# Hard-max attention on one core: the order of the first loads and the way the first transposes leave PSUM

## Chip, cores and metric

One of the eight cores of a Trainium2 chip runs the kernel. The metric is the device time of one execution in microseconds. A ratio is the mean time of one kernel's fast runs over the mean of the other's of the same rounds, so it is not quite the ratio of the medians that are quoted beside it; the bracket behind a ratio is its 95% interval.

The engines are called by their short names: PE multiplies matrices into the memory PSUM, ACT, DVE and POOL work on tiles, ACT and DVE copy results out of PSUM here, and POOL also issues the loads. The head is the time up to the first fold (explained below), the ramp the few tiles after it, the body the long stretch in which DVE is nearly always busy, the tail what follows the last fold. A landing is the moment at which a load has arrived.

## The reference, cut to what matters

```python
B, Sq, Sk, D = 4, 4096, 4096, 128            # all float32
def reference(q, k, v):
    logits = np.matmul(q, k.transpose(0, 2, 1))
    best = np.argmax(logits, axis=-1)         # one key per query
    return v[b_idx, best, :]
```

For each of 16,384 queries the kernel finds the key with the largest dot product and returns that key's row of v.

## The kernel before

The 16,384 queries are 128 tiles of 128. For each tile PE multiplies the transposed queries (`qT`) with the transposed keys (`kT`), in fp16. The keys stand in groups of four, and `kT` holds sums and differences of neighbours: `u` = 0 and 2 are sums, 1 and 3 differences. So |difference| + sum gives the larger of a pair (doubled), and 4096 keys shrink to 1024 group bounds. Per tile ACT takes two absolute values out of PSUM (`A`) and one scaled ReLU (`E`). DVE folds the last part with `E` into `W` (the fold) and then takes the eight largest. Later stages gather the three differences of the best group, decide between its four keys, and gather v.

q and k are loaded with a cast from fp32 to fp16, transposed by PE against an identity and copied out of PSUM. The identity is made on POOL, its fp16 forms `identh` and `identn` (its negative) on DVE. Before that PE runs warm-up matmuls on zeros, while the first loads are under way.

```python
pp = tc.tile_pool(name="ps", bufs=4, space=PSUM)      # four buffers of 1024 fp32 columns, for everything
# ... (cut)
for h in range(2):
    load_k(0, h, 0, 16)          # 2048 keys each, 512 KB written
load_q(0, 0, 8)                  # 8 query tiles
load_q(0, 8, NQT)                # the other 24
# ... 16 warm-up matmuls, make_identity, identh, identn (cut)
for h in range(2):
    put_k(0, h)                  # DVE: differences to the first key of each group; store of 384 KB as k16
# ... constants: three long iotas on POOL, iota_r, then on DVE:
nc.vector.tensor_copy(out=iota_h, in_=iota_r)

def trn_half(b, u, h):           # 8 matmuls of 128 columns
    # ... ps = tk_t[u], one 1024-column tile for both halves; o = ps[:, h * 512 + m * P: ...]
    if h == 1:
        nc.scalar.activation(out=kT[b % 2][:, u * 1024:(u + 1) * 1024], in_=ps, func=AF.Copy)

for u in (1, 3, 0, 2):
    trn_half(0, u, 0)            # fills all four PSUM buffers
trn_half(0, 1, 1)
trn_q(0, 0)                      # eight transposes and one 1024-column copy on ACT
trn_half(0, 3, 1)
trn_half(0, 0, 1)
dpart(0, 0)                      # pd = qT * kT[1]; ACT: A = |pd|
trn_half(0, 2, 1)
dpart(0, 1)
```

Each engine has its own instructions in this program order, and in the timelines below it works through them in that order.

Of the kernel before, what the change touches and what calls it, by code (L numbers as in the profile page):

```python
# [7 lines left out]
FP32 = mybir.dt.float32  # L8
# [8 lines left out]
AF = mybir.ActivationFunctionType  # L17
# [10 lines left out]
def kernel(ctx, tc, q, k, v, out):  # L28
    nc = tc.nc
    B, Sq, D = q.shape  # L30
    Sk = k.shape[1]
    P = 128
    NQT = Sq // P
# [10 lines left out]
    pp = ctx.enter_context(tc.tile_pool(name="ps", bufs=4, space=bass.MemoryType.PSUM))  # L44
# [10 lines left out]
    kT = [bp.tile([P, Sk], FP16, name=f"kT{i}", tag=f"kT{i}") for i in range(2)]  # L55
    qT = [bp.tile([P, Sq], FP16, name=f"qT{i}", tag=f"qT{i}") for i in range(2)]
    natk = [bp.tile([P, 2, 16, P], FP16, name=f"natk{i}", tag=f"natk{i}") for i in range(2)]
    kd = bp.tile([P, 2, 4, 3, P], FP16, name="kd", tag="kd")
    natq = [bp.tile([P, NQT, P], FP16, name=f"natq{i}", tag=f"natq{i}") for i in range(2)]

    def load_k(b, h, x, y):
        kb = k[b].rearrange("(h p n) d -> p h n d", p=P, n=16)
        nc.gpsimd.dma_start(out=natk[b % 2][:, h, x:y], in_=kb[:, h, x:y])  # L63

    def load_q(b, x, y):
        nc.gpsimd.dma_start(out=natq[b % 2][:, x:y], in_=q[b].rearrange("(p t) d -> p t d", p=P)[:, x:y])  # L66

    def put_k(b, h):
        if b >= B:
            return  # L70
        src = natk[b % 2][:, h].rearrange("p (g f) d -> p g f d", f=4)
        nc.vector.tensor_tensor(out=kd[:, h], in0=src[:, :, 1:4, :], in1=src[:, :, 0:1, :].to_broadcast([P, 4, 3, P]),
                                op=OP.subtract)
        kb16 = k16[b].rearrange("(h p n) d -> p h (n d)", p=P, n=4)
        nc.sync.dma_start(out=kb16[:, h], in_=kd[:, h].rearrange("p g f d -> p (g f d)"))

    def load_part(b, i):
        if b >= B:
            return
        if i < 8:  # L80
            load_k(b, i // 4, i % 4 * 4, i % 4 * 4 + 4)
        else:
            load_q(b, (i - 8) * NQT // 8, (i - 7) * NQT // 8)

    for h in range(2):
        load_k(0, h, 0, 16)
    load_q(0, 0, 8)
    load_q(0, 8, NQT)

    wz = cp.tile([P, 512], FP16, tag="wz")  # L90
    nc.vector.memset(wz, 0.0)
    for i in range(2):
        ps = pp.tile([P, 1024], FP32, tag="u", name=f"warm_{i}")
        for j in range(8):
            nc.tensor.matmul(out=ps[:, (j % 2) * 512:(j % 2 + 1) * 512], lhsT=wz[:, 0:P], rhs=wz, start=True, stop=True)

    ident = cp.tile([P, P], FP32, tag="ident")
    masks.make_identity(nc, ident)
    identh = cp.tile([P, P], FP16, tag="identh")
    nc.vector.tensor_copy(out=identh, in_=ident)  # L100
    identn = cp.tile([P, P], FP16, tag="identn")
    nc.vector.tensor_scalar(out=identn, in0=ident, scalar1=-1.0, scalar2=None, op0=OP.mult)
    for h in range(2):
        put_k(0, h)
    D_t = [cp.tile([P, 8, 4], FP32, name=f"D{i}", tag=f"D{i}") for i in range(3)]
    for D in D_t:
        nc.vector.memset(D, 0.0)
# [33 lines left out]

    tk_t = {}

    def trn_half(b, u, h):
        x = 2 * (u // 2)
        if h == 0:
            tk_t[u] = pp.tile([P, 1024], FP32, tag="u", name=f"tk_{b}_{u}")
        ps = tk_t[u]
        for m in range(4):
            o = ps[:, h * 512 + m * P:h * 512 + (m + 1) * P]  # L150
            nc.tensor.matmul(out=o, lhsT=natk[b % 2][:, h, 4 * m + x, :], rhs=identh, start=True, stop=False)
            nc.tensor.matmul(out=o, lhsT=natk[b % 2][:, h, 4 * m + x + 1, :],
                             rhs=identn if u % 2 else identh, start=False, stop=True)
        if h == 1:
            nc.scalar.activation(out=kT[b % 2][:, u * 1024:(u + 1) * 1024], in_=ps, func=AF.Copy)

    def unit_k(b, i):
        h, u, y = i // 8, i // 2 % 4, i % 2
# [10 lines left out]
    def turn_q(b, x, y):  # L169
        nc.sync.dma_start_transpose(out=qT[b % 2][:, x * P:y * P].rearrange("p (t r) -> p t r", r=P),  # L170
                                    in_=natq[b % 2][:, x:y, :].rearrange("p t d -> p (t d)"))

    def trn_q(b, g):
        if b >= B:
            return
        ps = pp.tile([P, 1024], FP32, tag="u", name=f"tq_{b}_{g}")
        for i in range(8):
            nc.tensor.matmul(out=ps[:, i * P:(i + 1) * P], lhsT=natq[b % 2][:, g * 8 + i, :], rhs=identh,
                             start=True, stop=True)
        nc.scalar.activation(out=qT[b % 2][:, g * 1024:(g + 1) * 1024], in_=ps, func=AF.Copy)  # L180

    E_t = {}
    A_t = {}
# [8 lines left out]
    def dpart(t, x):  # L192
        if t >= T:
            return
        ps = pp.tile([P, 1024], FP32, tag="u", name=f"pd_{t}_{x}")
        mm(ps, t, 1 + 2 * x, True)
        A = ep.tile([P, 1024], FP16, tag=f"A{x}", name=f"A_{t}_{x}")
        nc.scalar.activation(out=A, in_=ps, func=AF.Abs)  # L198
        A_t[t, x] = A
# [16 lines left out]
    def screen(t):  # L216
        dpart(t, 0)
        spart(t - 1, 0)
        dpart(t, 1)
        spart(t - 1, 1)  # L220

    def fold(t):
        E, ps = E_t.pop(t)
        nc.vector.scalar_tensor_tensor(out=W_t[t % NW].bitcast(I16)[:, 1::2], in0=ps, scalar=QSCALE, in1=E,  # L224
                                       op0=OP.mult, op1=OP.max)

    def top(t):
        nc.vector.max(out=TOP[:, t, :], in_=W_t[t % NW].bitcast(FP32))  # L228
# [338 lines left out]
    def all_rows():  # L567
# [4 lines left out]
        with tc.If(left > 0):  # L572
            for b in range(B):
                with tc.For_i(0, NQT, 1) as t:
# [13 lines left out]
                    nc.gpsimd.indirect_dma_start(out=vv, out_offset=None, in_=v_flat, in_offset=IOA(ap=win, axis=0))  # L588
                    nc.sync.dma_start(out=out[b].rearrange("(p t) d -> p t d", p=P)[:, bass.ds(t, 1), :].rearrange("p o d -> p (o d)"), in_=vv)

    for u in (1, 3, 0, 2):
        trn_half(0, u, 0)
    trn_half(0, 1, 1)
    trn_q(0, 0)
    trn_half(0, 3, 1)
    trn_half(0, 0, 1)
    dpart(0, 0)
    trn_half(0, 2, 1)
    dpart(0, 1)
    cuts = list(range(0, T - 16 + 1, 8)) + [T - x for x in (12, 8, 4, 0)]  # L600
    chunks = list(zip(cuts[:-1], cuts[1:]))
# [28 lines left out]
    def step(it):  # L630
        waiting = [s for s in live if s["kind"] == "dots" and ready(s, it)]
        quota = 2 if len(waiting) > 1 else 1
        for s in list(live):
            if s["kind"] == "dots":
                if quota and advance(s, it, False):
                    quota -= 1
            else:
                advance(s, it, False)
# [11 lines left out]
    def issue(it):  # L650
        n = 0
        while near_q and (n < 1 or near_q[0] in marks):
            g = near_q.pop(0)
            n += g not in marks
            g()
        if fast and it >= rest[0]:
            fast.pop(0)()
            rest[0] = it + 3
        take_late(2 if n == 0 and len(late_q) > 4 or it >= T - 8 and it % 2 else 1)

    def gathers(t):
        for c, (t0, t1) in enumerate(chunks):
            if t0 <= t < t1 and ((t - t0) % 2 or t == t1 - 1):
                x = t0 + (t - t0) // 2 * 2
                gather(c, x, t - x + 1)
            if t == t0:
                start(pick(c, t0, t1), "pick", c)
        if t % 8 == 7:
            put_rec(t - 7, t + 1)
        if t == SEGS[1] - 1:  # L670
            last = [c for c, x in enumerate(chunks) if x[1] == t + 1][0]
            start(flag_segment(0, t + 1, lambda: ("cnt", last) in done, lambda: ("out", last) in done), "flags")

    units = []
    for b in range(1, B):
        x = b * NQT
        units += [(x - 1, x - NQT + 8 + 3 * i // 2, unit_k, b, i) for i in range(16)]
    for it in range(T):
        b, qt = it // NQT, it % NQT
        if 2 <= qt < 10:  # L680
            load_part(b + 1, qt - 2)
        elif 10 <= qt < 18:
            load_part(b + 1, qt - 2)
        open_units = [u for u in units if u[1] <= it]
        if open_units:
            u = min(open_units)
            units.remove(u)
            assert it <= u[0]
            u[2](*u[3:])
        if it in (1, 2, 3):  # L690
            turn_q(0, it * 8, it * 8 + 8)
        elif qt >= 16 and qt % 2 == 0 and b + 1 < B:
            turn_q(b + 1, (qt - 16) * 2, (qt - 14) * 2)
        if it > 0:
            screen(it)
        if it >= 1:
            fold(it - 1)
        if it % NQT in (9, 13):
            put_k(it // NQT + 1, it % NQT // 13)
        step(it)  # L700
        if it >= 2:
            top(it - 2)
        if it >= 3:
            gathers(it - 3)
        step(it)
        issue(it)
# [72 lines left out]
```

## Time and profile before

| | before |
|---|---|
| median of 4 runs | 474.54 us (474.13 to 474.59) |
| span of the profiled run | 472.4 us |
| first `A` on ACT, first `E` on ACT, first fold on DVE | 14.79, 18.40, 19.53 us |
| last (128th) fold | 419.06 us |

First, the table of engines by stretch of the kernel before. After the stretch and its length come busy microseconds and instruction counts (x) of PE, PEld, DVE, ACT and POOL, then the granted clock, the DMA share and GB/s.

```profile
12.00:24.00 12.00, 10.48 (x63) 4.89 (x61) 3.02 (x3) 11.94 (x14) 0.95 (x2) 1.00 1.02 204
...
36.00:100.00 64.00, 61.46 (x310) 28.03 (x310) 63.03 (x107) 63.49 (x80) 34.47 (x40) 1.00 0.45 89
100.00:200.00 100.00, 91.48 (x444) 40.66 (x442) 98.31 (x175) 93.24 (x110) 72.75 (x81) 1.00 0.54 115
200.00:300.00 100.00, 89.65 (x443) 40.09 (x442) 98.17 (x193) 90.95 (x109) 71.27 (x79) 1.00 0.53 113
300.00:400.00 100.00, 90.61 (x394) 37.62 (x393) 100.00 (x208) 91.80 (x99) 69.53 (x70) 1.00 0.30 86
```

The second stretch belongs to the head: ACT is busy 11.94 of 12 us and DVE 3.02. From 36 to 100 us ACT and DVE are both nearly full, and from 100 us on DVE is busy 98 to 100%. So the head is paced by ACT and what feeds it, and the body by DVE.

Now the head by time. The timeline of ACT in the kernel before gives start and duration in us, line, operation and shapes; in brackets stand the idle time before it and what ended it.

```profile
9.87 1.02 ACT L155 ACTIVATE kT<-tk 128x1024 f16<-128x1024 f32 x1 [7.85 <-PE tk L152]
12.06 1.02 ACT L180 ACTIVATE qT<-tq 128x1024 f16<-128x1024 f32 x1 [1.17 <-PE tq L178]
12.98 1.94 ACT L155 ACTIVATE kT<-tk 128x1024 f16<-128x1024 f32 x2
14.79 1.04 ACT L198 ACTIVATE A<-pd 128x1024 f16<-128x1024 f32 x1
15.69 1.06 ACT L155 ACTIVATE kT<-tk 128x1024 f16<-128x1024 f32 x1
...
18.40 1.10 ACT L211 ACTIVATE E<-psn 128x1024 int16<-128x1024 f32 x1
```

And from the timelines of PE and of DVE in the same run:

```profile
11.40 0.62 PE L178 MATMUL tq<-identh,natq 128*128 128x128 f16 x8 [1.57 <-DMA natq<-in_q_dram]
```
```profile
6.60 0.96 DVE L72 TENSOR_TENSOR kd<-natk 128x1536 f16<-128x1536 f16 x1 [1.01 <-DMA natk<-in_k_dram]
9.01 1.05 DVE L72 TENSOR_TENSOR kd<-natk 128x1536 f16<-128x1536 f16 x1 [1.45 <-DMA natk<-in_k_dram]
...
10.10 1.29 DVE L126 CAST iota_h<-iota_r 128x128 f16<-128x128 f32 x1
19.53 1.31 DVE L224 SCALAR_TENSOR_TENSOR W<-psn,E 128x1024 int16<-128x1024 f32 x1 [8.14 <-ACT E L211]
```

k half 1 is there at 9.01 (the second DVE line waited for its landing). PE then waits for q until 11.40. From 12.06 ACT never rests: qT, three copies of 1024 columns, and the first `A` before the last of them. Five copies of about 1 us each pass through ACT, four of them after q's landing. DVE does nothing for 8.14 us before its first fold.

### The profile page before, as it was taken

How to read it: one execution, taken by the hardware profiler on the slowest of the kernel's cores; microseconds unless marked ns; L12 is line 12 of the kernel's file. 1: busy time of each engine (PE TensorE's matmuls, PEld its weight loads, DVE VectorE, ACT ScalarE, POOL GpSimd, SP SyncE). 2: the span in 40 equal slices, each digit the busy share in tenths (PEclk: the TensorE clock that was granted, in tenths of full speed). 3: DMA queues.
4: the chain of work that ended last, by engine and by line, in shares of the span. 5: the costliest groups of instructions: out<-in, count | busy, mean ns of one | idle time of the engine just before them, and what ended most of it. 6: DMA issues, size and time to landing. Idle time of an engine off the chain costs nothing. (4 is left out here: it accounts for less than half of the span.)

```text
span 472.4 us, 6274 instructions
## 1 busy us (share of the span) xinstructions
PE 381.7 (81%) x1840; PEld 168.9 (36%) x1840; DVE 417.8 (88%) x845; ACT 380.7 (81%) x438; POOL 305.6 (65%) x345
## 2 busy tenths in 40 slices
PE   7899999999898889999888979999999889920000
PEld 4444444443343334443333434443333333300000
DVE  4288999999999999999999999999999999998400
ACT  1999999999998899999998889999999888920000
POOL 9025544666787876666878765667777567777740
PEclk9999999999999999999999999999999999975555
DMA  7914564143455946242666736142333132324320
GB/s 134 211 32 87 108 115 93 56 119 63 119 94 125 193 87 147 57 124 65 134 133 156 113 108 97 55 114 65 118 89 109 52 94 58 110 73 121 98 82 5
DMA packets 40777, 47.43 MB, mean 100 GB/s; under 512 B 24200, under 2 KB 32395, under 8 KB 40736
## 3 DMA queue, kind: packets, MB, share of 16 engines
q0 software_dynamic: 18464, 30.97, 31.1%
q1 hardware_dynamic: 22272, 16.00, 12.8%
q8 instruction: 15, 0.25, 0.2%
q14 instruction: 26, 0.21, 0.2%
HBM read 39.59 MB, written 12.19 MB: 110 GB/s over the span
## 5 line engine op out<-in xcount | busy, mean ns | idle before, releaser
L198 ACT ACTIVATE A<-pd 128x1024 f16<-128x1024 f32 x256 | 259.1, 1046 | 18.3 <-PE pd L189 17.8
L245 POOL DMA_INDIRECT kg<-k,cand x128 | 127.2, 994 | 103.9 <-DVE p L264 25.0
L224 DVE SCALAR_TENSOR_TENSOR W<-psn,E 128x1024 int16<-128x1024 f32 x128 | 166.4, 1300 | 15.1 <-ACT E L211 12.1
L189 PE MATMUL pd<-kT,qT 128*128 128x512 f16 x512 | 152.1, 378 | 17.4 <-ACT A L198 15.5
L189 PE MATMUL psn<-kT,qT 128*128 128x512 f16 x512 | 151.8, 377 | 15.4 <-ACT A L198 10.8
L189 PEld LDWEIGHTS <-qT 128*128 128x128 f16 x1024 | 98.4, 97 | 166.1 <-issue 77.9
L228 DVE MAX8 TOP<-W 128x8 f32<-128x1024 f32 x128 | 156.2, 1220 | 0.0
L208 PE MATMUL psn<-A,identh 128*128 128x512 f16 x512 | 152.0, 378 | 0.0
L302 POOL DMA_INDIRECT vr<-in_v_dram,win x128 | 125.5, 980 | 39.0 <-issue 35.0
L211 ACT ACTIVATE E<-psn 128x1024 int16<-128x1024 f32 x128 | 132.8, 1038 | 6.7 <-PE psn L208 5.9
L208 PEld LDWEIGHTS <-identh 128*128 128x128 f16 x512 | 49.5, 97 | 60.8
L260 DVE TENSOR_TENSOR prod<-kg,natq 128x768 f16<-128x768 f16 x64 | 35.0, 549 | 1.5 <-DMA kg<-k,cand 1.5
L264 DVE TENSOR_TENSOR p<-prod 128x384 f16<-128x384 f16 x64 | 22.3, 350 | 0.0
L269 DVE TENSOR_REDUCE D<-p 128x6 f32<-128x192 f16 x64 | 21.4, 338 | 0.0
L167 ACT ACTIVATE kT<-uk 128x256 f16<-128x256 f32 x48 | 20.0, 416 | 0.9 <-PE uk L164 0.9
L163 PE MATMUL uk<-identh,natk 128*128 128x128 f16 x96 | 15.8, 218 | 0.6 <-ACT A L198 0.6
L63 POOL DMA_DIRECT2D natk<-in_k_dram x26 | 15.7, 604 | 0.9 <-POOLq L763 0.8
L267 DVE TENSOR_TENSOR p<-p 128x192 f16<-128x192 f16 x64 | 15.7, 247 | 0.0
L66 POOL DMA_DIRECT2D natq<-in_q_dram x26 | 15.4, 594 | 0.1
L460 PE MATMUL fp_e<-n_e,tri 128*128 128x1 f32 x2 | 0.6, 362 | 16.4 <-DVE n_e L458 16.4
L164 PEld LDWEIGHTS <-natk 128*128 128x128 f16 x96 | 9.3, 97 | 7.7 <-issue 5.5
L163 PEld LDWEIGHTS <-natk 128*128 128x128 f16 x96 | 9.3, 97 | 5.6
(148 smaller groups left out, 142.4 us busy)
## 6 DMA issues: line engine op xcount, KB each, us to landing
out_dram<-vr SPq DMA_DIRECT2D x14, 512.0 KB, 3.2
k<-kd SPq DMA_DIRECT2D x8, 384.0 KB, 4.5
natk<-in_k_dram POOLq DMA_DIRECT2D x24, 128.0 KB, 3.8
natq<-in_q_dram POOLq DMA_DIRECT2D x24, 128.0 KB, 3.3
kg<-k,cand POOLq DMA_INDIRECT x128, 2.7
vr<-in_v_dram,win POOLq DMA_INDIRECT x128, 2.5
natk<-in_k_dram POOLq DMA_DIRECT2D x2, 512.0 KB, 7.0
out_dram<-vr SPq DMA_DIRECT2D x4, 256.0 KB, 2.3
```

The costliest lines, as they stand in the source:

```text
L163: nc.tensor.matmul(out=o, lhsT=natk[b % 2][:, h, 4 * m + x, :], rhs=identh, start=True, stop=False)
L189: nc.tensor.matmul(out=ps[:, n * 512:(n + 1) * 512], lhsT=qT[b % 2][:, qt * P:(qt + 1) * P], rhs=kT[b % 2][:, u * 1024 + n * 512:u * 1024 ...
L198: nc.scalar.activation(out=A, in_=ps, func=AF.Abs)
L208: nc.tensor.matmul(out=ps[:, n * 512:(n + 1) * 512], lhsT=identh, rhs=A[:, n * 512:(n + 1) * 512], start=False, stop=True)
L211: nc.scalar.activation(out=E, in_=ps, func=AF.Relu, scale=QSCALE)
L224: nc.vector.scalar_tensor_tensor(out=W_t[t % NW].bitcast(I16)[:, 1::2], in0=ps, scalar=QSCALE, in1=E, op0=OP.mult, op1=OP.max)
L228: nc.vector.max(out=TOP[:, t, :], in_=W_t[t % NW].bitcast(FP32))
L245: near_q.append(lambda j=j: nc.gpsimd.indirect_dma_start(out=kg[:, j].rearrange("p f d -> p (f d)"), out_offset=None, in_=k16[t0 // NQT], ...
L260: nc.vector.tensor_tensor(out=prod, in0=kg, in1=natq[b % 2][:, x - b * NQT:x - b * NQT + m, :].unsqueeze(2).to_broadcast([P, m, 3, P]), op ...
L264: nc.vector.tensor_tensor(out=p1, in0=prod[:, :, :, 0:64], in1=prod[:, :, :, 64:128], op=OP.add)
L269: nc.vector.tensor_reduce(out=d[:, x - c0:x - c0 + m, 1:4], in_=p2, axis=AX_X, op=OP.add)
L302: late_q.append(lambda j=j: nc.gpsimd.indirect_dma_start(out=vr[:, j, :], out_offset=None, in_=v_flat, in_offset=IOA(ap=win[:, j:j + 1], a ...
```

## The change

Its intent: let the first tile's scores start earlier. Only four query tiles stay in the first q load, and it comes between the two halves of k. Each half of a key column block leaves PSUM by itself, as 512 columns, on ACT or on DVE. The second store of key differences moves behind the first fold, and two warm-up matmuls go.

```diff
-    for h in range(2):
-        load_k(0, h, 0, 16)
-    load_q(0, 0, 8)
-    load_q(0, 8, NQT)
+    load_k(0, 0, 0, 16)
+    load_q(0, 0, 4)
...
-        for j in range(8):            # per warm-up tile, two tiles
+        for j in range(7):
...
     masks.make_identity(nc, ident)
+    load_k(0, 1, 0, 8)
+    load_k(0, 1, 8, 16)
+    load_q(0, 4, 8)
+    load_q(0, 8, NQT)
...
-    for h in range(2):
-        put_k(0, h)
...
-    for u in (1, 3, 0, 2):
-        trn_half(0, u, 0)
-    trn_half(0, 1, 1)
-    trn_q(0, 0)
-    trn_half(0, 3, 1)
-    trn_half(0, 0, 1)
-    dpart(0, 0)
-    trn_half(0, 2, 1)
-    dpart(0, 1)
+    trn_half(1, 0, ALL, by_act)       # each: 512 columns, copied out at once
+    trn_half(3, 0, ALL, by_dve)
+    trn_half(0, 0, ALL, by_act)
+    trn_q(0, 4, by_dve)
+    trn_half(2, 0, ALL, by_act)
+    put_k(0, 0)
+    for u in (1, 3, 0, 2):
+        trn_half(u, 1, (0, 1))        # first part of k half 1
+    trn_half(1, 1, (2, 3), by_act)
+    trn_half(3, 1, (2, 3), by_dve)
+    dpart(0, 0)
+    trn_half(0, 1, (2, 3), by_dve)
+    trn_half(2, 1, (2, 3), by_dve)
+    dpart(0, 1)
...                                    # in the loop over tiles, at tile 1:
+            turn_q(0, 4, 8)            # the q tiles 4 to 7, by a DMA transpose
+            put_k(0, 1)                # behind the first fold
```

More of the change, by code (lines that the diff above doesn't have):

```diff
@@ L142, with trn_half, by_act, by_dve @@
     tk_t = {}
-    def trn_half(b, u, h):
+    def trn_half(u, h, ms, put=None):
         x = 2 * (u // 2)
-        if h == 0:
-            tk_t[u] = pp.tile([P, 1024], FP32, tag="u", name=f"tk_{b}_{u}")
+        if ms[0] == 0:
+            tk_t[u] = pp.tile([P, 512], FP32, tag="u", name=f"tk_{u}_{h}")
         ps = tk_t[u]
-        for m in range(4):
-            o = ps[:, h * 512 + m * P:h * 512 + (m + 1) * P]
-            nc.tensor.matmul(out=o, lhsT=natk[b % 2][:, h, 4 * m + x, :], rhs=identh, start=True, stop=False)
-            nc.tensor.matmul(out=o, lhsT=natk[b % 2][:, h, 4 * m + x + 1, :],
+        for m in ms:
+            o = ps[:, m * P:(m + 1) * P]
+            nc.tensor.matmul(out=o, lhsT=natk[0][:, h, 4 * m + x, :], rhs=identh, start=True, stop=False)
+            nc.tensor.matmul(out=o, lhsT=natk[0][:, h, 4 * m + x + 1, :],
                              rhs=identn if u % 2 else identh, start=False, stop=True)
-        if h == 1:
-            nc.scalar.activation(out=kT[b % 2][:, u * 1024:(u + 1) * 1024], in_=ps, func=AF.Copy)
+        if put is not None:
+            put(kT[0][:, u * 1024 + h * 512:u * 1024 + h * 512 + 512], ps)
+    def by_act(dst, src):
+        nc.scalar.activation(out=dst, in_=src, func=AF.Copy)
+    def by_dve(dst, src):
+        nc.vector.tensor_copy(out=dst, in_=src)
     def unit_k(b, i):
@@ L171, in turn_q, with trn_q @@
                                     in_=natq[b % 2][:, x:y, :].rearrange("p t d -> p (t d)"))
-    def trn_q(b, g):
-        if b >= B:
-            return
-        ps = pp.tile([P, 1024], FP32, tag="u", name=f"tq_{b}_{g}")
-        for i in range(8):
-            nc.tensor.matmul(out=ps[:, i * P:(i + 1) * P], lhsT=natq[b % 2][:, g * 8 + i, :], rhs=identh,
+    def trn_q(x, y, put):
+        ps = pp.tile([P, 512], FP32, tag="u", name=f"tq_{x}")
+        for i in range(x, y):
+            nc.tensor.matmul(out=ps[:, (i - x) * P:(i - x + 1) * P], lhsT=natq[0][:, i, :], rhs=identh,
                              start=True, stop=True)
-        nc.scalar.activation(out=qT[b % 2][:, g * 1024:(g + 1) * 1024], in_=ps, func=AF.Copy)
+        put(qT[0][:, x * P:y * P], ps)
     E_t = {}
@@ L589, in all_rows @@
                     nc.sync.dma_start(out=out[b].rearrange("(p t) d -> p t d", p=P)[:, bass.ds(t, 1), :].rearrange("p o d -> p (o d)"), in_=vv)
-    for u in (1, 3, 0, 2):
-        trn_half(0, u, 0)
-    trn_half(0, 1, 1)
-    trn_q(0, 0)
-    trn_half(0, 3, 1)
-    trn_half(0, 0, 1)
+    ALL = range(4)
+    trn_half(1, 0, ALL, by_act)
[4 more added lines that the diff above has]
+    put_k(0, 0)
+    for u in (1, 3, 0, 2):
+        trn_half(u, 1, (0, 1))
+    trn_half(1, 1, (2, 3), by_act)
+    trn_half(3, 1, (2, 3), by_dve)
     dpart(0, 0)
-    trn_half(0, 2, 1)
+    trn_half(0, 1, (2, 3), by_dve)
+    trn_half(2, 1, (2, 3), by_dve)
     dpart(0, 1)
@@ L689 @@
             u[2](*u[3:])
+        if it == 1:
+            turn_q(0, 4, 8)
         if it in (1, 2, 3):
@@ L697 @@
             fold(it - 1)
+        if it == 1:
+            put_k(0, 1)
         if it % NQT in (9, 13):
```

## The prediction

> **What bounds the kernel now.** The engine table by stretch: from 36 to 100 us ACT is busy 63.5 and DVE 63.0 of 64 us; from 100 to 400 us DVE is busy 98.3, 98.2 and 100 us of each 100, ACT 91 to 93, PE about 90. DVE sets the pace nearly to the end; a fixed tail (410 to 472 us) follows. The change touches only the head, so it is worth the amount by which the first tiles start earlier; that carries to the end, because DVE's work after its first fold stays the same.
>
> **The head before (timeline).** k half 0 has landed by 6.6 us, half 1 by 9.0, the first eight q tiles by 11.4. q is the last landing that matters: its transposes run at 11.40, ACT copies qT at 12.06, then three kT of 1024 columns (1.0 us each). From 12.06 ACT has no gap. First A at 14.79, first E 18.40, first fold on DVE 19.53.
>
> **What the change does.**
> - Only 4 q tiles (128 KB written) stand ahead of k half 1. At the observed 218 GB/s that is an estimated 0.6 us: q lands near 7.2, k half 1 near 9.7, and the k16 stores (at 7.6 before) no longer share the DMA engines with q.
> - Two warm-up matmuls fewer, 0.43 us each; transposes start near 6.7, not 7.4.
> - ACT loses its five 1024-column copies and gets four of 512 (estimated 0.62 us, between the measured 1.02 for 1024 and 0.42 for 256), one of them after half 1. DVE gets five of 512 (estimated 0.7 us, from the 1.30 of the 1024-column fold out of PSUM).
> - put_k(0,1), 1.0 us of DVE, moves behind the first fold, where DVE idled 1.44 us. Free.
>
> **What eats part of it.** In the instruction order DVE's iota_h cast stands ahead of the first DVE copy and waits for POOL's iota_r. That ran at 8.23; two more DMA issues (0.57 us each) now precede it, so about 9.4, and the cast ends near 9.9, later if POOL holds the port. The Trainium skill, "SBUF — State Buffer", section "Who interferes with whom", says that casts contend with GpSimd for a shared port; this trace agrees: the casts took 1.28 and 1.29 us, ending as POOL's iota and memset ended. So kT(3) half 0 leaves PSUM at 10.6, qT at 11.3, kd ends at 12.3, the half-1 copies on DVE near 13.1, 13.8, 14.5. PE's half-1 transposes wait for two of those PSUM buffers, until 11.4. Then ACT copies kT(1): first A near 13.1, first E 15.9, first fold 17.0.
>
> **Sum.** First fold about 2.5 us earlier; without the iota_h block about 4. All tiles follow at the old pace. Predicted 472.0 us; 470.4 to 473.6 should hold it 8 times in 10. Faster by over 2%: 0.01; within: 0.98; slower: 0.01.
>
> **What will show it.** First A, E and fold near 13, 16 and 17; DVE idle before its first kT copy, and that copy right behind iota_h; later stretches shifted alike, DVE still 98 to 100% busy from 100 to 400 us; ACT's busy total lower by about 2.5 us, DVE's higher by about 3.5.
>
> **What would make it wrong.** iota_h held longer by POOL's memsets (gain under 1 us). iota_h not blocking (gain 4 us). The second k store, now behind q's transposes on the SP queue, landing after about 28 us and delaying the first gathers. DVE's gather waits, or the tail's chain, swallowing the gain.

## The result, and the profile after

| | before | after |
|---|---|---|
| median of 4 runs | 474.54 us | 471.90 us (471.83 to 472.19) |
| ratio | | 0.9947 (0.993 to 0.9965) |
| span of the profiled run | 472.4 us | 470.1 us |
| first `A`, first `E`, first fold | 14.79, 18.40, 19.53 | 12.91, 15.63, 16.85 |
| last fold | 419.06 | 416.44 |

ACT's timeline in the changed kernel:

```profile
7.46 0.60 ACT L158 ACTIVATE kT<-tk 128x512 f16<-128x512 f32 x1 [5.43 <-PE tk L152]
8.35 1.27 ACT L158 ACTIVATE kT<-tk 128x512 f16<-128x512 f32 x2 [0.30 <-PE tk L152]
11.63 0.60 ACT L158 ACTIVATE kT<-tk 128x512 f16<-128x512 f32 x1 [2.02 <-PE tk L152]
12.91 2.86 ACT L202 ACTIVATE A<-pd 128x1024 f16<-128x1024 f32 x3 [0.68 <-PE pd L193]
15.63 1.05 ACT L215 ACTIVATE E<-psn 128x1024 int16<-128x1024 f32 x1
```

Three of ACT's four copies are done by 9.6 us, before k half 1 is of any use, and one copy of 0.60 us is left after it. Before, four copies of 1 us stood between k half 1 and the first `A`, and a fifth behind it; now one stands there, then the first `A`. The DVE timeline of the same run shows who took the rest:

```profile
9.51 0.48 DVE L126 CAST iota_h<-iota_r 128x128 f16<-128x128 f32 x1 [5.84 <-POOL iota_r L116]
9.65 0.68 DVE L161 CAST kT<-tk 128x512 f16<-128x512 f32 x1
10.25 0.68 DVE L161 CAST qT<-tq 128x512 f16<-128x512 f32 x1
10.85 0.95 DVE L72 TENSOR_TENSOR kd<-natk 128x1536 f16<-128x1536 f16 x1
11.85 0.69 DVE L161 CAST kT<-tk 128x512 f16<-128x512 f32 x1
13.13 1.29 DVE L161 CAST kT<-tk 128x512 f16<-128x512 f32 x2 [0.58 <-PE tk L152]
16.85 1.31 DVE L228 SCALAR_TENSOR_TENSOR W<-psn,E 128x1024 int16<-128x1024 f32 x1 [2.43 <-PE psn L212]
18.05 0.94 DVE L72 TENSOR_TENSOR kd<-natk 128x1536 f16<-128x1536 f16 x1
19.46 1.31 DVE L228 SCALAR_TENSOR_TENSOR W<-psn,E 128x1024 int16<-128x1024 f32 x1 [0.46 <-ACT E L215]
```

DVE starts its first kT copy right behind the `iota_h` cast, which waited for POOL until 9.51, as predicted. PE's timeline names the two waits on its way to k half 1 (a landing, then a PSUM buffer that DVE had to empty):

```profile
9.76 0.23 PE L151 MATMUL tk<-identh,natk 128*128 128x128 f16 x1 [0.78 <-DMA natk<-in_k_dram]
...
10.99 0.22 PE L151 MATMUL tk<-identh,natk 128*128 128x128 f16 x1 [0.21 <-DVE qT L161]
...
12.28 0.59 PE L193 MATMUL pd<-kT,qT 128*128 128x512 f16 x2 [0.46 <-ACT kT L158]
```

The body in the table of engines by stretch, to be held against the lines of before:

```profile
36.00:100.00 64.00, 61.83 (x317) 28.26 (x315) 63.44 (x109) 63.12 (x79) 34.03 (x40) 1.00 0.48 89
100.00:200.00 100.00, 90.96 (x440) 40.51 (x439) 98.21 (x174) 93.16 (x112) 71.18 (x81) 1.00 0.59 114
200.00:300.00 100.00, 90.02 (x442) 40.06 (x440) 98.17 (x197) 91.29 (x109) 70.03 (x78) 1.00 0.57 114
300.00:400.00 100.00, 90.37 (x392) 37.51 (x391) 99.81 (x206) 91.73 (x99) 69.03 (x71) 1.00 0.31 86
```

DVE is as full as before. So the gain should be a plain shift, and it can be followed tile by tile. The table gives the start of the n-th fold in the trace of each run, less that of the kernel before in its trace.

| run | tile 0 | tile 1 | tile 8 | tile 32 | tile 64 | tile 96 | tile 127 | ratio of times |
|---|---|---|---|---|---|---|---|---|
| after | -2.68 | -2.82 | -2.82 | -2.79 | -2.83 | -2.74 | -2.62 | 0.9947 |
| after, run again | -2.69 | -2.83 | -2.84 | -2.81 | -2.84 | -2.78 | -2.62 | 0.9949 |
| `load_only` | +1.43 | +1.43 | +1.43 | +1.41 | +1.45 | +1.45 | +1.42 | 1.0018 |
| `evict_only` | -1.19 | -1.33 | -1.34 | -1.34 | -1.36 | -1.27 | -1.13 | 0.9991 |
| `evict_clean` | +0.68 | +0.54 | +0.53 | +0.54 | +0.52 | +0.54 | +0.50 | 0.9998 |
| `cast_late` | -2.88 | -3.02 | -3.03 | -3.02 | -3.01 | -2.95 | -2.80 | 0.9949 |
| `warm_16` | -2.68 | -2.82 | -2.82 | -2.79 | -2.84 | -2.82 | -2.63 | 0.9947 |
| `delay_head` | -1.37 | -1.55 | -1.70 | -1.69 | -1.71 | -1.64 | -1.43 | 0.9976 |
| `delay_fold` | -2.67 | -0.56 | -2.66 | -2.67 | -2.66 | -2.60 | -2.48 | 0.9949 |
| `delay_body` | -2.68 | -2.82 | -2.83 | -2.86 | -0.11 | -0.82 | -0.70 | 0.9996 |
| `k_first` | -3.28 | -3.28 | -3.29 | -3.25 | -3.27 | -3.30 | -3.33 | 0.9935 |

What the head gives, the last tile still has: 2.68 us at tile 0, 2.62 at tile 127, 2.64 between the medians. The experiments ask what in the head gave it.

### The profile page after: what moved, and what is told of

It reads as the page before. It is cut to its first block, busy times and chain, and to the rows that moved or that the text cites. A ratio compares the mean times of both kernels' runs of the same rounds, so it can differ in the third digit from the quotient of the medians.

```text
span 470.1 us, 6272 instructions
## 1 busy us (share of the span) xinstructions
PE 380.3 (81%) x1834; PEld 168.7 (36%) x1834; DVE 418.7 (89%) x850; ACT 378.5 (81%) x437; POOL 303.3 (65%) x347
## 5 line engine op out<-in xcount | busy, mean ns | idle before, releaser
L249 POOL DMA_INDIRECT kg<-k,cand x128 | 124.8, 975 | 105.4 <-DVE p L268 27.8
L66 POOL DMA_DIRECT2D natq<-in_q_dram x27 | 15.9, 591 | 0.1
```

What stands on the lines that cost most here:

```text
L249: near_q.append(lambda j=j: nc.gpsimd.indirect_dma_start(out=kg[:, j].rearrange("p f d -> p (f d)"), out_offset=None, in_=k16[t0 // NQT], ...
```

## The experiments

Ratios are to the kernel before, run in the same rounds on the same chip. Every run had 5 rounds.

### 1. The load order alone

```diff
 kernel before, with
-    load k half 0, k half 1, q 0..8, q 8..32
+    load k half 0, q 0..4, (identity), k half 1 in two, q 4..8, q 8..32
+    trn_q of four tiles, 512 columns on ACT;  turn_q(0, 4, 8) at tile 1
```

> The kernel before with the load order of the changed kernel alone (k half 0, four q tiles, identity, k half 1 in two, the rest of q); eviction as before: 1024 columns on ACT once both halves are there, both k16 stores early. Theory A (the gain comes from taking copies off ACT's path between k half 1 and the first A): the first A stays near 14.5 us, the first fold near 19.2, the time within 0.5 us of before (474.0 to 474.5). Rival (the gain comes from q landing early): first A near 13, about 472.5 us.

Measured: 475.94 us against 475.08, ratio 1.0018 (1.0005 to 1.0031); first `A` at 16.23, first fold at 20.96 us. With the old eviction this order makes the kernel slower. The timelines of PE and of ACT in this run:

```profile
9.90 0.23 PE L153 MATMUL tk<-identh,natk 128*128 128x128 f16 x1 [1.28 <-DMA natk<-in_k_dram]
...
11.22 0.29 PE L153 MATMUL tk<-identh,natk 128*128 128x128 f16 x1 [0.92 <-DMA natk<-in_k_dram]
...
11.40 0.31 PE L153 MATMUL tk<-identh,natk 128*128 128x128 f16 x1
11.51 0.31 PE L154 MATMUL tk<-identn,natk 128*128 128x128 f16 x1
12.94 0.58 PE L180 MATMUL tq<-identh,natq 128*128 128x128 f16 x4 [1.11 <-ACT kT L157]
```
```profile
11.86 1.02 ACT L157 ACTIVATE kT<-tk 128x1024 f16<-128x1024 f32 x1 [9.84 <-PE tk L154]
13.56 0.60 ACT L182 ACTIVATE qT<-tq 128x512 f16<-128x512 f32 x1 [0.67 <-PE tq L180]
14.41 1.94 ACT L157 ACTIVATE kT<-tk 128x1024 f16<-128x1024 f32 x2 [0.26 <-PE tk L154]
16.23 1.03 ACT L200 ACTIVATE A<-pd 128x1024 f16<-128x1024 f32 x1
```

k half 1 lands in two parts at 9.90 and 11.22 us, where it was whole at 9.01 before, and the 1024-column copies can only start after it. q's transposes wait too, until ACT's first copy has emptied a PSUM buffer. Theory A expected a head that stays where it was; in fact it moved back by 1.43 us.

But not all of the 1.43 us is the later landing. From 11.0 to 17.8 us the granted clock is 0.50 in this run, and the transposes start 0.107 us apart (11.40, 11.51), not 0.055. An estimate from these timelines: at full clock the four transposes ahead of the first copy would end 0.21 us sooner, q's four would take 0.39 us (as in the changed kernel) and not 0.58, and ACT's wait of 0.26 us at 14.41 would go. So about 0.7 of the 1.43 us is the half clock, and about 0.8 the landing. The mean clock is 0.936 to 0.939 in all five runs, against 0.939 to 0.945 in the eleven of the kernel before, so the profiled run is hardly alone in it. No run took the two apart. The rival, that early q makes the gain, falls either way: the first `A` would still come at about 15.6, and it expected 13.

### 2. The eviction alone

```diff
 changed kernel, with
-    load k half 0, q 0..4, (identity), k half 1 in two, q 4..8, q 8..32
+    load k half 0, k half 1, q 0..4, (identity), q 4..8, q 8..32
```

> The changed kernel with the loads in the old order (both k halves, then q, with four q tiles as the first q load); eviction by half key columns on two engines kept. Theory A: most of the gain stays: first A 12.5 to 13.5 us, first fold 16.5 to 17.5, 471.7 to 472.5 us. Rival (load order): first A near 14.5, about 474 us.

Measured: 474.64 us against 475.08, ratio 0.9991 (0.9978 to 1.0004), whose interval includes 1; first `A` at 14.39, first fold at 18.34 us. That fits Theory A nowhere; the first `A` and the time are near what the rival expected, but the first fold comes 1.19 us earlier. Theory A fell here, in the form that the eviction carries the gain whatever the loads do. But the run had an accident. From the timeline of DVE, then that of POOL:

```profile
3.72 0.23 DVE L101 CAST identh<-ident 128x128 f16<-128x128 f32 x1 [2.58 <-POOL ident masks.py:199]
3.86 4.85 DVE L103 TENSOR_SCALAR identn<-ident 128x128 f16<-128x128 f32 x1
```
```profile
3.64 1.08 POOL L66 DMA_DIRECT2D natq<-in_q_dram  x2
4.72 3.67 POOL L110 IOTA W<- 128x1024 uint16 x3
```

`identn` stood 4.85 us on DVE while POOL issued two DMAs and ran three iotas, and PE, after one transpose, went on only at 8.76 us. So the run did not measure the eviction alone. Runs 3 and 4 take the accident away.

### 3. The eviction alone, with identn on ACT

```diff
 evict_only, with
-    nc.vector.tensor_scalar(out=identn, in0=ident, scalar1=-1.0, ...)
+    nc.scalar.activation(out=identn, in_=ident, func=AF.Copy, scale=-1.0)
```

> The eviction alone with the old load order, as before, but with identn made on ACT, so that POOL cannot hold it up (in the first run of this kind it took 4.85 us and half 0 was transposed 1.9 us late). Theory (that form is limited by PE's order, in which q's transposes, with q landing near 10.4 us, stand ahead of the fourth half-0 transpose and all of half 1): hardly better, first fold 17.9 to 18.3. Rival (the held-up identn spoiled it, and the eviction alone has the whole gain): first fold near 16.8, ratio 0.995 or less.

Measured: 474.79 us against 474.20, ratio 0.9998 (0.9982 to 1.0015); first fold at 20.21 us. The first fold became later than in run 2, which no theory had expected; the time is that of the kernel before. PE's timeline, and the table of engines by stretch, show what happened:

```profile
11.14 0.53 PE L181 MATMUL tq<-identh,natq 128*128 128x128 f16 x4 [3.04 <-DMA natq<-in_q_dram]
11.47 0.31 PE L150 MATMUL tk<-identh,natk 128*128 128x128 f16 x1
```
```profile
8.00:11.00 3.00, 0.11 (x2) 0.00 (x0) 0.83 (x2) 0.60 (x1) 3.00 (x14) 1.00 0.98 110
...
12.00:13.00 1.00, 0.96 (x9) 0.80 (x8) 1.00 (x2) 0.43 (x1) 1.00 (x3) 0.50 1.01 209
13.00:14.00 1.00, 0.78 (x8) 0.78 (x8) 0.27 (x1) 0.16 (x1) 0.34 (x1) 0.50 1.10 228
```

With half 0 transposed by 8.1 us, q's transposes are next in PE's order. q lands at 11.14 here, so PE idles 3.04 us although k half 1 lies ready (run 10, with the same loads, transposes it from 8.93). Then it runs at a granted clock of 0.50: the 128-column transposes start 0.107 us apart, not 0.055.

### 4. The same with PE kept busy

```diff
 evict_clean, with
+    ten matmuls of 512 columns on zeros, into a PSUM tile of their own
     trn_q(0, 4, by_dve)
```

> The run before (eviction alone, old load order, identn on ACT) with ten dummy matmuls of 512 columns ahead of q's transposes, where PE had idled 3.04 us and then ran at a granted clock of 0.50 from 12 to 14 us. If that half clock made its first fold late (20.21 us): no clock under 1.00 and the first fold 1.3 to 1.8 us earlier, 18.4 to 18.9. Rival (q's landing at 11.1 us alone): first fold within 0.4 us of 20.21.

Measured: this run fell on a chip where the kernel before took 512.83 us (508.81 to 553.79), so its time (505.51 us; ratio on that chip 0.9866, 0.9806 to 0.9927) is compared with nothing here; 512.83 is the median of all eleven runs, three of them slow. Only its head is read. Up to tile 32 its folds keep one distance (1.39 to 1.41 us from tile 1 on) to those of the kernel before on the first chip, so the head runs there as elsewhere: the clock stays at 1.00, q's transposes run at 10.88, the first fold at 18.27 us, 1.94 earlier than in run 3 (1.3 to 1.8 were expected). The half clock was the cause of most of it; 0.26 us is q's earlier landing. So the new eviction with k ahead of q is worth 1.26 us at the first fold (19.53 to 18.27). The accident of run 2 had kept PE's idle time ahead of q short (0.29 us, with q's transposes at 10.50), so its clock stayed at 1.00, and that is why it hid itself.

"Alone" needs a word, for runs 2 to 4 keep the small first q load of the change. q's transposes run at 10.88 here and at 11.40 in the kernel before, and from them to the first `A` it takes 3.45 us here and 3.39 before. So the 0.46 us by which the first `A` is earlier go with q's earlier start, and that moves by itself: PE waited for the same small load until 10.50, 11.14 and 10.88 us in runs 2, 3 and 4. What the eviction brings for certain lies behind the first `A`: from it to the first `E` it takes 2.73 us and not 3.61, because no kT copy stands between them on ACT any more.

### 5. The iota_h cast out of the way

```diff
 changed kernel, with
-    nc.vector.tensor_copy(out=iota_h, in_=iota_r)      # among the constants
     ...
     trn_half(2, 1, (2, 3), by_dve)
+    nc.vector.tensor_copy(out=iota_h, in_=iota_r)
```

> The changed kernel with DVE's iota_h cast moved behind its last kT copy. The prediction put the cost of that cast, standing ahead of the first DVE copy, at 1.5 us (first fold about 15.4, 470.4 us). Rival, from the changed kernel's trace: k half 1 lands at 9.7 us, only 0.6 us before the PSUM buffers come free, so the gain is 0.5 to 0.7 us: first A near 12.3, first fold near 16.2, 471.3 us.

Measured: 472.46 us against 475.08, ratio 0.9949 (0.9937 to 0.9961); first fold at 16.65 us, 0.20 earlier than in the changed kernel. PE's timeline says why it is not 1.5 us:

```profile
9.69 0.23 PE L150 MATMUL tk<-identh,natk 128*128 128x128 f16 x1 [0.31 <-DMA natk<-in_k_dram]
...
10.99 0.23 PE L150 MATMUL tk<-identh,natk 128*128 128x128 f16 x1 [0.24 <-DMA natk<-in_k_dram]
```

DVE's first copy now runs at 8.03 rather than 9.65. But PE then waits for the second part of k half 1 until 10.99 us, the very time at which the changed kernel's PE got its last PSUM buffer from DVE. The time shows none of the 0.20 us (run 6, in the same rounds, has 0.9947). Two waits stood side by side, and taking one away leaves the other.

### 6. Sixteen warm-up matmuls

```diff
 changed kernel, with
-        for j in range(7):
+        for j in range(8):
```

> The changed kernel with 16 warm-up matmuls instead of 14. The prediction counted 0.43 us each. If they are on the path: first fold 0.86 us later, 472.8 us. Rival: PE's transposes of half 0 would end near 9.6 us, still ahead of the landing of k half 1 at 9.7, so nothing: first fold at 16.85 within 0.1, 471.9 us.

Measured: 472.47 us against 475.08, ratio 0.9947 (0.9935 to 0.996); first fold at 16.85 us, as in the changed kernel. Two warm-ups fewer bring nothing: half 0 is transposed before k half 1 lands either way.

### 7 to 9. The same DVE work in three places

```diff
 changed kernel, with
+    pad = cp.tile([P, 1280], FP32); nc.vector.memset(pad, 0.0); nc.vector.memset(pad, 1.0)
 delay_head: ahead of the last two kT copies on DVE
 delay_fold: behind the first fold and put_k(0, 1)
 delay_body: at tile 60
```

> The changed kernel with two memsets of 1280 fp32 columns on DVE (about 1.33 us each, from 0.27 us for 256) ahead of its last two kT copies. If the end follows the first fold one for one: first fold about 2.0 to 2.5 us later than 16.85, and the time over the changed kernel's by the same amount within 0.3 us (ratio to before near 0.9995). Rival (the ramp's idle time takes it up): under 1 us.

> The same two memsets behind the first fold and the second k16 subtraction. DVE idles 0.46 us there and 0.2 to 0.33 us per tile until about 31 us. If DVE idle time after the first fold takes work up (the prediction's word free for put_k): cost 0.3 to 1.3 us of the 2.67. Rival (DVE bound from its first fold on): 2.2 us or more.

> The same two memsets at tile 60, where DVE is 98% busy. If DVE sets the pace there: the time over the changed kernel's by 2.2 to 2.7 us (ratio to before near 1.000). Rival (ACT, 91 to 93% busy, or PE sets it): under 1 us.

Measured, against 474.37 us of before: `delay_head` 473.37, ratio 0.9976 (0.9963 to 0.999); `delay_fold` 471.97, ratio 0.9949 (0.9935 to 0.9962); `delay_body` 474.19, ratio 0.9996 (0.9982 to 1.0009). The changed kernel itself has 0.9949 on this chip.

- In the head the first fold comes 1.31 us later. I had expected 2.0 to 2.5; a memset took 1.12 us, and the copies behind it had slack. Those 1.31 us arrive at the end: 1.19 at tile 127, and (0.9976 - 0.9949) * 474.4 = 1.3 us in the time. That is the one-for-one carry, shown by moving the head the other way.
- Behind the first fold the second fold comes 2.26 us later, and by tile 8 all but 0.16 us is made up. The time does not change, where 0.3 to 1.3 us had been expected. DVE's idle time in the ramp is real, so `put_k(0, 1)` was free there.
- At tile 60 the delay is 2.73 us at tile 64 and still 1.92 at tile 127; in the time it is (0.9996 - 0.9949) * 474.4 = 2.2 us. There DVE sets the pace.

### 10 and 11. Both k halves first, q last in PE's order

```diff
 changed kernel, with
-    load k half 0, q 0..4, (identity), k half 1 in two, q 4..8, q 8..32
+    load k half 0, k half 1, q 0..4, (identity), q 4..8, q 8..32
-    identn on DVE
+    identn on ACT
+    trn_half(1, 0, ALL, by_act); trn_half(3, 0, ALL, by_dve); trn_half(0, 0, ALL, by_act); trn_half(2, 0, ALL, by_dve)
+    trn_half(1, 1, ALL, by_act); trn_half(3, 1, ALL, by_dve); trn_half(0, 1, ALL, by_dve); trn_half(2, 1, ALL, by_dve)
+    trn_q(0, 4, by_act)
+    dpart(0, 0); dpart(0, 1); put_k(0, 0); put_k(0, 1); iota_h       # no put_k at tile 1
```

> Both k halves load first and four q tiles after them, eviction by half key columns kept, and nothing waits in line for q: PE transposes q last, ACT copies qT; identn is made on ACT (its DVE form stood 4.85 us behind POOL in the run with the old load order); iota_h and both k16 subtractions stand behind the last copy. Theory (the changed kernel is limited by the landing of k half 1, which its own load order moved from 9.0 to 10.95 us): q lands near 10.45, first A near 12.0, first fold near 16.0, ratio to before 0.9925, 1 us better than the changed kernel. Rival (the load order of the change is what makes the gain): first A at 13 or later, ratio 0.995 or more.

Measured: 471.18 us against 474.37, ratio 0.9935 (0.9922 to 0.9949); first `A` at 12.45, first fold at 16.25 us.

```profile
9.59 0.60 ACT L156 ACTIVATE kT<-tk 128x512 f16<-128x512 f32 x1 [0.53 <-PE tk L150]
11.15 0.60 ACT L156 ACTIVATE qT<-tq 128x512 f16<-128x512 f32 x1 [0.97 <-PE tq L180]
12.45 2.85 ACT L200 ACTIVATE A<-pd 128x1024 f16<-128x1024 f32 x3 [0.70 <-PE pd L191]
```

The last copy before the first `A` is now qT. The gain over the changed kernel is 0.6 us at the first fold, a little more than half of the forecast 1 us, because the first `A` comes at 12.45 and not at 12.0. It was run again beside the changed kernel:

> The changed kernel once more, beside the next run on one chip: ratio to before 0.994 to 0.996.

> The kernel with both k halves first and q behind, once more: first folds 0.5 to 0.6 us ahead of the changed kernel's, the median 0.4 to 0.9 us below it. Rival (its better median was the chip's): within 0.2 us.

Measured on one chip, with 474.20 us for before: the changed kernel 471.99 us (471.75 to 472.29), ratio 0.9949 (0.9937 to 0.9962); this one 471.25 us (471.20 to 471.45), ratio 0.9935 (0.9922 to 0.9949). All its five runs lie below all six of the changed kernel, and its first fold is at 16.33 us against 16.84. It beats both kernels, by 0.7 us in the median over the changed one; the intervals of the two ratios overlap, the runs and the folds do not. It has the old order of k and q, so the load order of the change is not needed for the gain. Run 4 has the same loads, but q ahead of k half 1 in PE's order, and its first fold is 2.02 us later (18.27 to 16.25). That speaks for letting PE's order and the order of landing agree; but this kernel also moved the `iota_h` cast and the k16 subtractions and gave qT to ACT, and no run took these apart.

## Why the prediction was right

It said 472.0 us, and 471.9 was measured. The main line held at the steps that were to show it: first `A` 13.1 (12.91), first `E` 15.9 (15.63), first fold 17.0 (16.85), a body that shifts as a whole with DVE 98 to 100% busy, and the second k store free. ACT's busy total fell by 2.2 us (380.7 to 378.5; predicted about 2.5).

Four smaller terms of it were wrong, and none of them moved the sum by much. For the first two that is partly luck: k half 1 was expected 1.3 us too early, and the wait for PSUM buffers behind the `iota_h` cast (until 11.4 in the prediction, 10.99 in the trace) ended at the moment at which it landed, and so hid it.

- "Without the iota_h block about 4." Run 5 gives 2.88 us at the first fold, not 4. The block costs 0.2 us, because the second part of k half 1 lands at 10.99.
- "k half 1 near 9.7." Its first part landed then, the second about 1.3 us later. I had laid the loads end to end at 218 GB/s; from 6.5 to 8 us, around the small q load, DMA moved 37 to 98 GB/s in the changed kernel, against 180 to 246 in the kernel before. Run 1 shows the price of this order under the old eviction: the first fold 1.43 us later, half clock included.
- "Two warm-up matmuls fewer, 0.43 us each." Run 6 gives nothing at the first fold.
- "DVE's [busy total higher] by about 3.5." It rose by 0.9 us (417.8 to 418.7). The five copies came to 3.3 us, but the casts of the identity and of `iota_h` lost some 1.8 us of waiting that the profile counts as busy: 1.36 us from 4.24 to 5.60 became 0.37, and 1.29 became 0.48. The remaining 0.6 us was not traced.

How the gain comes about rests on runs. At the first fold the load order under the old eviction costs 1.43 us (some 0.7 of it the half clock, by the estimate in run 1), the eviction under the old order of k and q saves 1.26 (0.5 of it with q's earlier start), and both together save 2.68. So they are not additive. Of the 2.68 us, 1.88 lie ahead of the first `A`, and neither part alone brings them; 0.89 lie between the first `A` and the first `E`, where the eviction took a copy off ACT; from there to the fold it takes 0.09 longer. With the old loads PE's order has q ahead of k half 1, and q lands last. With the new loads q is there when its turn comes (PE transposed it at 8.15 us without waiting). The price is a later k half 1, and there the half-column copies pay: one 0.60 us copy on ACT, not four of 1 us, stands between it and the first `A`.

Two things stay open. `evict_only` gained 1.13 us at its last fold but only 0.4 us in its time (0.0009 of 475): in its profiled run the stretch from the last fold to the end took 55.0 us, against 53.3 in the kernel before and 53.7 in the changed one, whose profiles came from other rounds. `cast_late`, in the same rounds but with the load order of the change, has 54.9 us there, and `load_only` 53.7, so the long tail does not follow the load order; what made it is not shown. And the six times of `evict_clean` fall into two groups (473.3 to 473.6, and 474.5 to 475.1). A half clock that sets in only in some executions would do that. Their mean clocks fit (0.945 and 0.946 in the short ones, 0.939 to 0.941 in the long ones), but those of the kernel before spread from 0.939 to 0.945 with no such groups in its times, and only one of the six was profiled.

## What to carry to other kernels

Before a saturated body, a microsecond saved in the head is a microsecond saved at the end, but only on the chain that starts the body: the same 2.2 us or so of DVE work cost 1.3, 0 and 2.2 us in three places. An engine that works in program order should find its operands landing in that order; judge a load order together with the order of the engine that consumes it, since either alone can cost time (runs 1 and 3). And when two waits end at nearly the same moment, count what the second leaves before crediting the removal of the first.

## What the Trainium skill lacked or had wrong

- "SBUF — State Buffer", section "Who interferes with whom": it says that of DVE in a two-port mode and GpSimd the one that issues first holds the shared pair "for the whole instruction", and the other blocks. The traces agree that casts and scalar multiplies on DVE block (1.28 us for a 128x128 cast), and that a subtraction of two SBUF operands beside a memset on POOL does not (0.95 us in the changed kernel, while POOL's memset ran from 10.73 to 12.15). What it lacks: as these traces read, the loser need not get the next turn. `identn` waited 4.85 us, through two DMA issues and three iotas on POOL, and the same instruction took 0.22 us in the changed kernel, where POOL was also issuing DMAs, but before its iotas.
- "TensorE: Matmul & The Clock Gate", Part 1: it puts the fall to half clock after at least one idle window of about 3.4 us. Here an idle time of 3.04 us was enough (run 3: clock 0.50 from 12 to 14 us, starts 0.107 us apart), and in run 1 two of 1.28 and 0.92 us with four matmuls between them (in the 3.4 us before the fall at 11.0 PE had worked about 1.4 us), while one of 1.57 us in the kernel before was not. So the longest gap does not decide. In both runs the fall came about 6.8 us after the warm-ups had gone over to full speed (near 4.2 and 4.4 us, estimated from their spacing), and the half clock lasted 6.8 and 3.4 us: multiples of 3.4, so the phase seems to matter, which no run varied. Its cold rate of 426.7 ns for 512 columns agrees with the warm-ups (0.43 us apart in the kernel before).
- No page has this of the profile: over the first 5 us the granted clock reads 1.00 in the kernel before, although the warm-ups start 0.43 us apart, twice the 0.22 us of the last two. This record of the clock does not cover the cold start, so read the spacing of the matmuls there.
